# A gMLP layer on one core: two of the seven Strassen products of a pair of strips are computed by a second level

## The chip, the core and the metric

The kernel runs on one core of a Trainium2 chip. A core has a matmul engine (TensorE; PE in the profile, PEld its weight loads), a vector engine (DVE), a scalar engine (ACT), GpSimd (POOL), a sync engine (SP) that issues transfers, 16 DMA engines, an on-chip memory SBUF and accumulator banks in PSUM. The metric is the device time of one execution in microseconds (us), the median over runs.

## What is computed

One layer of the reference (DEPTH is 1, so only the first mixer runs), in float32, with x 1024 x 2048, E = 4096 inner channels, w_in 2048 x 12288, w_out 4096 x 2048:

```python
h = rmsnorm(x, g_in)
u, v, gate = split(h @ w_in, 3, axis=-1)
v = rmsnorm(gelu(v), v_gain)
vc = v.reshape(1, 8, 128, 8, 512)               # chunks of 128 positions, 8 groups of 512 channels
sv = einsum('gpq,bnqgc->bnpgc', w_s, vc) + b_s
y = gelu(u) * sv
out = rmsnorm(x + (y * silu(gate)) @ w_out, fnorm)
```

## The kernel before, in words

**Strassen.** h @ w_in is cut into 12 strips of two column groups of 512: strips 0 to 3 hold v (E columns, two groups each), strips 4 to 11 hold group g of u and group g of gate. A strip is a product of 2 x 2 blocks: rows of the 1024 positions in two halves, the 2048 input channels in two halves, the two column groups. It is done with 7 products in place of 8 (`IN_ORDER`; `A_OF` and `B_OF` name the sums of blocks of h and of w that a product takes). Each product is 4 *steps* of 256 input channels. A step combines and splits its weights in `feed`: `w_sum` (L112, vector engine, where two blocks are summed), `w_hi` (L88, scalar engine, the rounded value), `w_lo` (L89, vector engine, the remainder). It then does 24 matmuls of 128x128 on 128x512: two halves `u` of the channels, four row blocks `m`, and three products hi-hi, hi-lo, lo-hi for each (`mm3`, L102 to L104).

**Loads.** Strip 0 makes the hi and lo parts of h and of its sums from x and writes them to `a_dram` through POOL's queue; every later strip reads two of them of 512 KB for each step, and each block of w once (16 of 512 KB a strip), all through SP's queue. `prefetch` runs `LOADS` = 3 steps ahead, `feed` runs `AHEAD` = 2 steps ahead. What is really resident is set by slots: tiles of 128 x 1024 floats in the pools `big` (w_raw, a_hi, a_lo), `hl` (six: w_hi and w_lo of three steps), `sum` (three) and `ax` (the rest).

**The end of a product.** `end_of` puts the work on the four PSUM banks of a product into the list `soon` (U = M1 - M2 - M5, outputs c11 to c22, gelu or silu by `act`), and the rest (squares and gains of v, transposes of y) into `later`; `work` puts some of both behind the matmuls of each step. Blocks 12 and 21 go straight from the bank through `act`. From strip 4 on, spatial mixing of a group (`spatial_step` k = 0 to 10: load v, split it, matmuls `sv`, `scalar_tensor_tensor` L370, transposes L398 and writes of y) is spread over products 7 and 6 of its strip (k = 0 to 7) and product 1 of the next (k = 8 to 10). After the strips the `out` stage multiplies y by w_out in the same way, one level of seven products. A scheduler sets the order of instructions on each engine from the order of the program and what each needs.

Of the kernel before, what the change touches and what calls it, by code (L numbers as in the profile page):

```python
# [23 lines left out]
FIRST_ORDER = (5, 3, 6, 1, 2, 4, 7)  # L24
OUT_ORDER = (3, 5, 2, 4, 1, 7, 6)
# [7 lines left out]
def gmlp_kernel(ctx, tc, x, xT, g_in, w_in, gain, wsT, bsT, w_out, fnorm, out):  # L33
# [19 lines left out]
    SLOTS = {"big": 25, "hl": 6, "sum": 3, "ax": 16}  # L53
# [65 lines left out]
    steps = [("in", s, p, j) for s in range(len(strips)) for p in (IN_ORDER if s else FIRST_ORDER) for j in range(JI)]  # L119
# [7 lines left out]

    wraw, yraw, wparts, aparts = {}, {}, {}, {}
    hx = {}

    def load_w(step, block, us=None):
        kind, s, p, j = step
        mat, cols, n = (w_in, strips, JI) if kind == "in" else (w_out, outs, JO)
        key = (kind, s, 0 if kind == "in" else p, block, j)
        if key not in wraw or us is not None:
            k = ((block // 10 - 1) * n + j) * 2 * P
            col = cols[s][block % 10 - 1]
            if key not in wraw:
# [73 lines left out]
    def feed(i):  # L212
# [16 lines left out]
        raw = combine(B_OF[p], lambda b: load_w(step, b), "sum", "w_sum")  # L229
# [25 lines left out]
    def load_x(jj, h, us=None):  # L255

        if (jj, h) not in hx:
            hx[jj, h] = slot("big", "x_t")
# [149 lines left out]

    def products(i, banks, fresh, ms=range(4)):
# [10 lines left out]

    def advance(i):
        prefetch(i + LOADS)
        feed(i + AHEAD)
# [5 lines left out]
    i = 0  # L429
    before = None  # L430
    for s in range(len(strips)):
        is_v = s < NV
        g = s - NV
        a = (s - 1) % 2
# [256 lines left out]
```

## Time and profile before

| | |
|---|---|
| median of 3 runs | 2521.28 us (2520.66 to 2523.06) |
| the profiled execution | 2521.24 us, of which the span of instructions is 2519.2 us |
| granted TensorE clock, mean | 0.998 |
| matmuls (PE) | 99% of the span, 10948 instructions |
| vector engine, scalar engine, POOL | 61%, 36%, 9% |
| transfers | 685.09 MB, 272 GB/s in the mean |

The busy share says how much of the span an engine had an instruction under way; for the engine that is near 100% its number of instructions sets the time, for the others the waits do, and only where somebody waits for them.

### The profile page before, as it was taken

The numbers are of one execution on the slowest core, as the hardware profiler recorded it, in microseconds if no ns is written. First come the engines' busy times: TensorE is split into PE (matmuls) and PEld (weight loads), VectorE is DVE, ScalarE is ACT, GpSimd is POOL, SyncE is SP. The second block draws the span as 40 slices with busy tenths as digits, with TensorE's granted clock in tenths as the row PEclk, the third lists the DMA queues.
The fourth block names the chain that finished last, engine by engine and source line by source line (L and its number), as shares of the span: only waits on it lengthen the run. The fifth ranks groups of instructions, "written<-read, shape, count | busy, mean of one in ns | idle before, by whom it ended". The sixth has DMA issues, their size and how long they took to land.

```text
span 2519.2 us, 28981 instructions
## 1 busy us (share of the span) xinstructions
PE 2489.9 (99%) x10948; PEld 2055.3 (82%) x10948; DVE 1526.9 (61%) x1561; ACT 898.2 (36%) x1148; POOL 219.2 (9%) x386
## 2 busy tenths in 40 slices
PE   8999999999999999999999999999999999999998
PEld 6778888888888888888888888888888888888886
DVE  7984544546456464564645646456468664676795
ACT  6752433324333242332423324233243342232342
POOL 2220000000001001010010100101002110010010
PEclk9999999999999999999999999999999999999999
DMA  9896977959677687776877768777689865788885
GB/s 384 289 352 220 346 252 253 340 189 378 239 293 246 221 326 245 291 250 220 328 244 292 250 221 327 242 291 252 215 334 305 289 217 187 218 269 282 304 285 190
DMA packets 242922, 685.09 MB, mean 272 GB/s; under 512 B 22736, under 2 KB 22752, under 8 KB 242784
## 3 DMA queue, kind: packets, MB, share of 16 engines
q1 hardware_dynamic: 202160, 541.13, 60.7%
q0 software_dynamic: 40624, 142.12, 15.3%
q8 instruction: 86, 1.41, 0.2%
q14 instruction: 52, 0.43, 0.1%
HBM read 611.86 MB, written 71.30 MB: 271 GB/s over the span
## 4 chain that ended last, share of the span: by engine, by line
PE 93%; DMA 2%; issue 2%; POOL 1%; DVE 1%; ACT 0%; SPq 0%; POOLq 0%; ACTq 0%
PE m L102 23%; PE m L104 23%; PE m L103 23%; PE o L102 8%; PE o L104 8%; PE o L103 8%; DMA w_raw<-in_w_in 2%; PE sv L104 1%; PE sv L102 1%; PE sv L103 1%; DMA x_t<-in_xT 0%; DMA v<-c 0%; SPq L261 0%; POOL rx L287 0%; ACT sq_o L563 0%
## 5 line engine op out<-in xcount | busy, mean ns | idle before, releaser
L102 PE MATMUL m<-w_hi,a_hi 128*128 128x512 f32 x2688 | 1047.4, 390 | 14.0 <-ACT a_hi L88 8.4
L103 PE MATMUL m<-w_lo,a_hi 128*128 128x512 f32 x2688 | 1047.7, 390 | 1.4 <-DVE w_lo L89 1.4
L104 PE MATMUL m<-w_hi,a_lo 128*128 128x512 f32 x2688 | 1046.7, 390 | 1.7 <-DVE a_lo L89 1.7
L88 ACT ACTIVATE w_hi<-w_sum 128x1024 fp32r<-128x1024 f32 x320 | 338.7, 1059 | 906.1 <-PE m L103 643.7
L89 DVE TENSOR_TENSOR w_lo<-w_sum,w_hi 128x1024 fp32r<-128x1024 f32 x320 | 391.4, 1223 | 440.5 <-ACT w_hi L88 440.0
L102 PEld LDWEIGHTS m<-w_hi,a_hi 128*128 128x128 f32 x2688 | 505.0, 188 | 122.3 <-ACT a_hi L88 10.1
L104 PEld LDWEIGHTS m<-w_hi,a_lo 128*128 128x128 f32 x2688 | 505.0, 188 | 108.6 <-DVE a_lo L89 3.4
L103 PEld LDWEIGHTS m<-w_lo,a_hi 128*128 128x128 f32 x2688 | 505.1, 188 | 107.4 <-DVE w_lo L89 1.8
L112 DVE TENSOR_TENSOR w_sum<-w_raw 128x1024 f32<-128x1024 f32 x320 | 389.8, 1223 | 161.8 <-DMA w_raw<-in_w_in 147.6
L102 PE MATMUL o<-w_hi,a_hi 128*128 128x512 f32 x896 | 348.7, 389 | 0.8 <-DVE o L638 0.8
L104 PE MATMUL o<-w_hi,a_lo 128*128 128x512 f32 x896 | 348.6, 389 | 0.0
L103 PE MATMUL o<-w_lo,a_hi 128*128 128x512 f32 x896 | 348.6, 389 | 0.0
L89 DVE TENSOR_TENSOR w_lo<-w_raw,w_hi 128x1024 fp32r<-128x1024 f32 (+1 forms) x129 | 156.3, 1215 | 237.9 <-ACT w_hi L88 237.8
L88 ACT ACTIVATE w_hi<-w_raw 128x1024 fp32r<-128x1024 f32 (+1 forms) x129 | 136.1, 1055 | 453.6 <-PE m L103 341.6
L102 PEld LDWEIGHTS o<-w_hi,a_hi 128*128 128x128 f32 x896 | 168.2, 188 | 36.3 <-DVE o L638 1.5
L104 PEld LDWEIGHTS o<-w_hi,a_lo 128*128 128x128 f32 x896 | 168.2, 188 | 34.9
L103 PEld LDWEIGHTS o<-w_lo,a_hi 128*128 128x128 f32 x896 | 168.2, 188 | 34.9
L403 POOL DMA_DIRECT2D y<-y_t x128 | 74.0, 586 | 409.4 <-DVE y_t L398 405.7
L155 POOL DMA_DIRECT2D y_raw<-y x96 | 50.9, 531 | 511.4 <-DVE w_sum L112 206.7
L95 ACT ACTIVATE a_hi<-a_sum 128x1024 fp32r<-128x1024 f32 x40 | 42.3, 1058 | 102.6 <-DVE a_sum L112 102.6
L450 ACT ACTIVATE c<-m,rx 128x512 f32<-128x512 f32 x92 | 57.8, 682 | 51.0 <-PE m L104 51.0
L479 DVE TENSOR_TENSOR u<-u,m 128x1024 f32<-128x1024 f32 x46 | 56.1, 1219 | 31.4 <-PE m L104 29.9
(94 smaller groups left out, 1148.3 us busy)
## 6 DMA issues: line engine op xcount, KB each, us to landing
w_raw<-in_w_out SPq DMA_DIRECT2D x192, 512.0 KB, 7.5
w_raw<-in_w_in SPq DMA_DIRECT2D x191, 512.0 KB, 6.2
y_raw<-y POOLq DMA_DIRECT2D x96, 512.0 KB, 6.7
a_hi<-a_0h SPq DMA_DIRECT2D x77, 512.0 KB, 6.3
a_lo<-a_0l SPq DMA_DIRECT2D x77, 512.0 KB, 5.3
a_hi<-a_1h SPq DMA_DIRECT2D x77, 512.0 KB, 6.0
a_lo<-a_1l SPq DMA_DIRECT2D x77, 512.0 KB, 5.0
a_hi<-a_2h SPq DMA_DIRECT2D x77, 512.0 KB, 6.1
```

Of the source, the lines that this page charges most:

```text
L88: nc.scalar.activation(out=hi, in_=raw, func=AF.Copy)
L89: nc.vector.tensor_tensor(out=lo, in0=raw, in1=hi.bitcast(F32), op=ALU.subtract)
L95: nc.scalar.activation(out=hv, in_=rv_, func=AF.Copy)
L102: nc.tensor.matmul(out=acc, lhsT=ah, rhs=bh, start=start, stop=False, skip_group_check=on)
L103: nc.tensor.matmul(out=acc, lhsT=ah, rhs=bl, start=False, stop=False, skip_group_check=on)
L104: nc.tensor.matmul(out=acc, lhsT=al, rhs=bh, start=False, stop=stop, skip_group_check=on)
L112: nc.vector.tensor_tensor(out=s, in0=a, in1=b, op=ALU.add if of[1] > 0 else ALU.subtract)
L155: nc.gpsimd.dma_start(out=yraw[key], in_=y_dram[g][block // 10 - 1][b * P:(b + 2) * P].rearrange("(p u) t -> p u t", p=P))
L403: nc.gpsimd.dma_start(out=yd[n, :, :, q * P:(q + 1) * P], in_=yts[0][n][q * Q:(q + 1) * Q])
L450: nc.scalar.activation(out=d[:, c], in_=src[:, c], func=AF.Gelu_apprx_tanh if is_v or n == 0 else AF.Silu, scale=rx[half][:, at:at + 1])
L479: soon.append((1.2, lambda t=t: nc.vector.tensor_tensor(out=cs["u"][t], in0=cs["u"][t], in1=banks[t], op=ALU.subtract)))
```

## The change

Strips 0 and 1 stay as they were. From strip 2 on, strips are taken in pairs. Product 2 is (A21 + A22) B11 and product 5 is (A11 + A12) B22; for the two strips of a pair the left sides are the same, so the two products of a pair are one product of a 512 x 1024 matrix with a 1024 x 1024 one. It is cut into quarters and done with seven products (`deep` steps, two for each of the seven, 12 matmuls a step, `deep_product`). Their hi and lo parts of quarters are made once, in strip 1 (`whole`, `deep_parts`), and written to `d_dram` (28 writes of 512 KB). The results D2 and D5 stay in SBUF (`ax`). Then each strip of the pair has its five other products in the order 1, 4, 3, 7, 6, and `end_of` adds D2 and D5 in SBUF on the vector engine. Loads run ahead by `when`, in which a deep step counts a half. Block 11 of w is loaded again for product 6. The steps 8 to 10 of a mixing left over from the strip before stand at the first deep steps of product 2.

```diff
+DEEP = (2, 5)
+REST_ORDER = (1, 4, 3, 7, 6)
...
-    SLOTS = {"big": 25, "hl": 6, "sum": 3, "ax": 16}
+    SLOTS = {"big": 21, "hl": 6, "sum": 3, "ax": 20}
...
-    steps = [("in", s, p, j) for s in range(len(strips)) for p in (IN_ORDER if s else FIRST_ORDER) for j in range(JI)]
+    steps = [("in", s, p, j) for s in range(2) for p in (IN_ORDER if s else FIRST_ORDER) for j in range(JI)]
+    for s in range(2, len(strips), 2):
+        steps += [("deep", s, (p, q), j) for p in DEEP for q in IN_ORDER for j in range(JI // 2)]
+        steps += [("in", s + n, p, j) for n in range(2) for p in REST_ORDER for j in range(JI)]
...
-        key = (kind, s, 0 if kind == "in" else p, block, j)
+        key = (kind, s, 0 if kind == "in" and not (s > 1 and (p, block) == (6, 11)) else p, block, j)
...
+    def load_deep(step, block):
+        _, s, (p, q), j = step
+        return load_w(("deep", s + block % 10 - 1, p, 2 * (block // 10 - 1) + j), 11 if p == 2 else 22)
...
-        if kind == "in" and s > 0:
+        if kind == "deep" and j > 0:
+            aparts[i] = aparts[i - 1]
+        elif kind == "deep" or (kind == "in" and s > 0):
             parts = [slot("big", f"a_{l}", F32R) for l in ("hi", "lo")]
-            for t, d in zip(parts, a_dram[p, j]):
+            for t, d in zip(parts, d_dram[p] if kind == "deep" else a_dram[p, j]):
...
-        for c, at in enumerate((0, 1, 4, 6)):
+        for c, at in enumerate((0, 1, 4, 5)):
             if k == at:
                 load_v(g, c)
-        for c, at in enumerate((2, 3, 6, 8)):
+        for c, at in enumerate((2, 3, 6, 7)):
             if k == at:
                 prepare_spatial(g, c)
...
+    def whole(i):
...
+        raws[p, j] = slot("ax", "a_raw")
+        hi, lo = aparts[i]
+        nc.vector.tensor_tensor(out=raws[p, j], in0=hi.bitcast(F32), in1=lo.bitcast(F32), op=ALU.add)
+    def deep_parts(p, q):
+        of = A_OF[q]
...
+        if len(of) > 1:
+            both = slot("sum", "d_sum").rearrange("p a (b c) -> p (a b) c", c=HT2)
+            for j in range(2):
+                nc.vector.tensor_tensor(out=both[:, 2 * j:2 * j + 2], in0=block(of[0], j), in1=block(of[2], j),
+                                        op=ALU.add if of[1] > 0 else ALU.subtract)
+            split(both, hi, lo)
+        else:
+            for j in range(2):
+                split(block(of[0], j), hi[:, 2 * j:2 * j + 2], lo[:, 2 * j:2 * j + 2])
+        for t, d in zip((hi, lo), d_dram[p, q]):
+            nc.gpsimd.dma_start(out=d.rearrange("p a (b c) -> p (a b) c", c=HT2), in_=t.bitcast(F32))
...
+    def deep_product(i, bank, fresh):
...
+        for u in range(2):
+            for m in range(2):
+                t = slice(m * P, (m + 1) * P)
+                mm3(bank[:, m], ah[:, 2 * j + u, t], al[:, 2 * j + u, t], bh[:, u], bl[:, u],
+                    fresh and j == 0 and u == 0, j == 1 and u == 1, not fresh)
+    when = [0.0]
+    for step in steps:
+        when.append(when[-1] + (0.5 if step[0] == "deep" else 1.0))
+    fetched, fed = [LOADS], [AHEAD]
     def advance(i):
-        prefetch(i + LOADS)
+        while fetched[0] < len(steps) and when[fetched[0]] <= when[i] + LOADS:
+            prefetch(fetched[0])
+            fetched[0] += 1
         feed(i + AHEAD)
...
+                for j in range(JI // 2):
+                    advance(i)
+                    if n == 0 and s > NV:
+                        at = {(1, 0): 8, (1, 1): 9, (2, 0): 10}.get((q, j))
+                        if at:
+                            spatial_step(at, *before)
+                    deep_product(i, bank, fresh)
+                    work(0.1 if j else 0)
+                    i += 1
+                end_deep(p, q, bank)
...
+    def end_deep(p, q, bank):
+        if q == 1:
+            deep["u"] = slot("ax", "d_u")
+            soon.append((0, lambda u=deep["u"]: nc.scalar.activation(out=u, in_=bank, func=AF.Copy)))
+        elif q in (2, 5):
+            soon.append((1.2, lambda u=deep["u"]: nc.vector.tensor_tensor(out=u, in0=u, in1=bank, op=ALU.subtract)))
+        elif q in (4, 3):
+            d = deep[p, 21 if q == 4 else 12] = slot("ax", f"d{p}")
+            soon.append((0, lambda: nc.scalar.activation(out=d, in_=bank, func=AF.Copy)))
+        else:
+            u = deep["u"]
+            d = deep[p, 11 if q == 7 else 22] = slot("ax", f"d{p}") if q == 7 else u
+            soon.append((1.2, lambda: nc.vector.tensor_tensor(out=d, in0=u, in1=bank, op=ALU.add)))
...
+                if s > 1:
+                    n = s % 2 + 1
+                    d2, d5 = deep[2, 10 * (t + 1) + n], deep[5, 10 * (t + 1) + n]
+                    if p == 1:
+                        for block, d in ((11, d5), (22, d2)):
+                            c = slot("ax", f"c{block}_{t}")
+                            cs.setdefault(block, []).append(c)
+                            soon.append((1.2, lambda t=t, c=c, d=d: nc.vector.tensor_tensor(
+                                out=c, in0=banks[t], in1=d, op=ALU.subtract)))
+                    else:
+                        block = {4: 21, 3: 12, 7: 11, 6: 22}[p]
+                        if p in (4, 3):
+                            cs.setdefault(block, []).append(d2 if p == 4 else d5)
+                        def add(t=t, block=block):
+                            c = cs[block][t]
+                            nc.vector.tensor_tensor(out=c, in0=c, in1=banks[t], op=ALU.add)
+                            act(block, t, c)
+                        soon.append((1.2, add))
...
+            if s == 1 and p in DEEP:
+                for q in IN_ORDER:
+                    later.append((2.3, lambda p=p, q=q: deep_parts(p, q)))
...
```

A pair of strips issues 56 loads of w and 108 of h parts, where it issued 32 and 112. TensorE has 10708 matmuls, 420 `w_sum` and 507 `w_hi`/`w_lo` are made in place of 320 and 447.

The vector engine's rows, before, at products 5 and 4 of a strip (out<-in; names end in a running number):

```order
L89 TENSOR_TENSOR w_lo_6017<-w_raw_5786,w_hi_6016 128x1024
L89 TENSOR_TENSOR w_lo_6049<-w_raw_5625,w_hi_6048 128x1024
L112 TENSOR_TENSOR w_sum_6220<-w_raw_6178,w_raw_5661 128x1024
L89 TENSOR_TENSOR w_lo_6081<-w_raw_5663,w_hi_6080 128x1024
L479 TENSOR_TENSOR u0_5974<-u0_5974,m2_0_5976 128x1024
L112 TENSOR_TENSOR w_sum_6256<-w_raw_6214,w_raw_5736 128x1024
L89 TENSOR_TENSOR w_lo_6115<-w_raw_5738,w_hi_6114 128x1024
L479 TENSOR_TENSOR u1_5975<-u1_5975,m2_1_5977 128x1024
L89 TENSOR_TENSOR w_lo_6151<-w_raw_5788,w_hi_6150 128x1024
L89 TENSOR_TENSOR w_lo_6187<-w_sum_6184,w_hi_6186 128x1024
```

and of the changed kernel in product 5 of a deep stage, where it sums and splits for deep steps:

```order
L116 TENSOR_TENSOR w_sum_10166<-w_raw_9990,w_raw_9848 128x1024
L536 TENSOR_TENSOR d_u_10031<-d_u_10031,d5_5_10074 128x1024
L93 TENSOR_TENSOR w_lo_10123<-w_sum_10120,w_hi_10122 128x1024
L116 TENSOR_TENSOR w_sum_10185<-w_raw_10013,w_raw_9875 128x1024
L93 TENSOR_TENSOR w_lo_10142<-w_sum_10139,w_hi_10141 128x1024
L116 TENSOR_TENSOR w_sum_10212<-w_raw_9846,w_raw_10033 128x1024
L93 TENSOR_TENSOR w_lo_10169<-w_sum_10166,w_hi_10168 128x1024
L116 TENSOR_TENSOR w_sum_10231<-w_raw_9873,w_raw_10056 128x1024
L93 TENSOR_TENSOR w_lo_10188<-w_sum_10185,w_hi_10187 128x1024
L116 TENSOR_TENSOR w_sum_10258<-w_raw_10158,w_raw_10160 128x1024
L93 TENSOR_TENSOR w_lo_10215<-w_sum_10212,w_hi_10214 128x1024
L116 TENSOR_TENSOR w_sum_10277<-w_raw_10204,w_raw_10206 128x1024
```

Before, a step of 24 matmuls stands for each `w_lo`, and most of these read a `w_raw`; after, a step of 12 stands for each, most have a `w_sum`, and each sum stands two `w_lo` ahead of its own (`w_lo_10123` and `w_lo_10142` stand between `w_sum_10166` and `w_lo_10169`).

The vector engine where the mixing of one strip ends beside the next strip, before (in product 1 of the next strip; `u` L508 is of the next strip's accumulations, L459 forms u times gate):

```order
L89 TENSOR_TENSOR w_lo_6873<-w_sum_6870,w_hi_6872 128x1024
L508 TENSOR_TENSOR u0_5974<-u0_5974,m5_0_6108 128x1024
L508 TENSOR_TENSOR u1_5975<-u1_5975,m5_1_6109 128x1024
L89 TENSOR_TENSOR w_lo_6923<-w_sum_6920,w_hi_6922 128x1024
L459 TENSOR_TENSOR c21_0_6396<-c21_0_6396,u0_5974 128x1024
L459 TENSOR_TENSOR c21_1_6397<-c21_1_6397,u1_5975 128x1024
L89 TENSOR_TENSOR w_lo_6973<-w_sum_6970,w_hi_6972 128x1024
L89 TENSOR_TENSOR w_lo_7005<-w_raw_6749,w_hi_7004 128x1024
L370 SCALAR_TENSOR_TENSOR c21_0_6396<-sv1_1_0_7008,bs_sb_65,c21_0_6396 128x512 x2
```

and of the changed kernel, where the next is deep product 2 (L575 forms u times gate, L396 the product with sv):

```order
L93 TENSOR_TENSOR w_lo_9652<-w_raw_9479,w_hi_9651 128x1024
L575 TENSOR_TENSOR d2_7549<-d2_7549,c22_0_8965 128x1024
L575 TENSOR_TENSOR d_u_7337<-d_u_7337,c22_1_8967 128x1024
L93 TENSOR_TENSOR w_lo_9678<-w_raw_9519,w_hi_9677 128x1024
L396 SCALAR_TENSOR_TENSOR d2_7549<-sv3_1_0_9706,bs_sb_65,d2_7549 128x512
L93 TENSOR_TENSOR w_lo_9702<-w_raw_9481,w_hi_9701 128x1024
L396 SCALAR_TENSOR_TENSOR d2_7549<-sv3_1_0_9706,bs_sb_65,d2_7549 128x512
L396 SCALAR_TENSOR_TENSOR d_u_7337<-sv3_1_1_9707,bs_sb_65,d_u_7337 128x512 x2
L424 STREAM_TRANSPOSE y_t0_9754<-d2_7549 128x8x32
L424 STREAM_TRANSPOSE y_t1_9755<-d2_7549 128x8x32
L424 STREAM_TRANSPOSE y_t0_9754<-d2_7549 128x8x32
L93 TENSOR_TENSOR w_lo_9739<-w_raw_9521,w_hi_9738 128x1024
```

Here `w_lo_9652` and `w_lo_9678` are for the two steps of quarter product 2, `w_lo_9702` and `w_lo_9739` for those of 5. The same mixing rows stand between `w_lo` of steps half as long.

The scalar engine at the end of a v strip, before (L450 gelu, L324 square with its sum):

```order
L88 ACTIVATE w_hi_3644<-w_sum_3642 128x1024
L450 ACTIVATE u0_2730<-u0_2730,rx1_75 128x512 x2
L450 ACTIVATE u1_2731<-u1_2731,rx1_75 128x512 x2
L324 ACTIVATE sq_v_3712,ssv_71<-u0_2730 128x512 x2
L324 ACTIVATE sq_v_3718,ssv_71<-u1_2731 128x512 x2
L88 ACTIVATE w_hi_3684<-w_sum_3682 128x1024
L88 ACTIVATE w_hi_3728<-w_raw_3505 128x1024
```

and of the changed kernel, at the end of strip 1 and the start of the first deep stage:

```order
L92 ACTIVATE w_hi_2695<-w_sum_2693 128x1024
L92 ACTIVATE w_hi_2761<-w_raw_2589 128x1024
L566 ACTIVATE u0_1700<-u0_1700,rx1_75 128x512 x2
L566 ACTIVATE u1_1701<-u1_1701,rx1_75 128x512 x2
L350 ACTIVATE sq_v_2741,ssv_71<-u0_1700 128x512 x2
L350 ACTIVATE sq_v_2747,ssv_71<-u1_1701 128x512 x2
L92 ACTIVATE w_hi_2779<-w_raw_2639 128x1024
L534 ACTIVATE d_u_2795<-d2_1_2754 128x1024
L92 ACTIVATE w_hi_2803<-w_raw_2591 128x1024
```

In both, four gelus and four squares stand between two `w_hi`. The `w_hi` behind them, `w_hi_3684` before, is for a step of 24 matmuls; `w_hi_2779` is for the fourth deep step of 12.

## Rows read from the trace of the kernel before

**Rows 1.** The page: span, busy time of each engine, bytes moved.
```profile
span 2519.2 us, 28981 instructions
...
PE 2489.9 (99%) x10948; PEld 2055.3 (82%) x10948; DVE 1526.9 (61%) x1561; ACT 898.2 (36%) x1148; POOL 219.2 (9%) x386
...
DMA packets 242922, 685.09 MB, mean 272 GB/s; under 512 B 22736, under 2 KB 22752, under 8 KB 242784
```

**Rows 2.** Windows: length, then PE, PEld, DVE, ACT, POOL busy; clock, DMA share, GB/s.
```profile
0.00:150.00 150.00, 134.51 (x561) 106.13 (x562) 132.51 (x147) 102.80 (x138) 35.21 (x65) 1.00 0.89 332
150.00:308.00 158.00, 156.43 (x691) 129.20 (x690) 89.95 (x87) 55.70 (x86) 8.61 (x17) 1.00 0.81 302
1398.00:1554.00 156.00, 156.00 (x690) 129.18 (x689) 87.73 (x96) 51.53 (x61) 11.40 (x20) 1.00 0.74 266
```

**Rows 3.** Groups, whole span: busy us, mean ns | idle before, what ended it.
```profile
L103 PE MATMUL m<-w_lo,a_hi 128*128 128x512 f32 x2688 | 1047.7, 390 | 1.4 <-DVE w_lo L89 1.4
```

**Rows 4.** Timeline, PE: start us, us, instruction; first matmuls of two steps.
```profile
1000.15 0.39 PE L102 MATMUL m<-w_hi,a_hi 128*128 128x512 f32 x1
...
1005.59 0.39 PE L102 MATMUL m<-w_hi,a_hi 128*128 128x512 f32 x1
```

**Rows 5.** Timeline, ACT, beside it: in brackets the idle time before, and its end.
```profile
1004.89 1.06 ACT L88 ACTIVATE w_hi<-w_sum 128x1024 fp32r<-128x1024 f32 x1 [4.38 <-PE m L103]
1010.33 1.06 ACT L88 ACTIVATE w_hi<-w_sum 128x1024 fp32r<-128x1024 f32 x1 [4.38 <-PE m L103]
```

**Rows 6.** Groups by shape, whole span (columns as in rows 3).
```profile
L89 DVE TENSOR_TENSOR w_lo<-w_sum,w_hi 128x1024 fp32r<-128x1024 f32 x320 | 391.4, 1223 | 440.5 <-ACT w_hi L88 440.0
L112 DVE TENSOR_TENSOR w_sum<-w_raw 128x1024 f32<-128x1024 f32 x320 | 389.8, 1223 | 161.8 <-DMA w_raw<-in_w_in 147.6 <-DMA w_raw<-in_w_out 8.7
...
L479 DVE TENSOR_TENSOR u<-u,m 128x1024 f32<-128x1024 f32 x46 | 56.1, 1219 | 31.4 <-PE m L104 29.9
...
L398 DVE STREAM_TRANSPOSE y_t<-c 128x256 f32<-128x256 f32 x128 | 43.6, 408 | 0.0
L370 DVE SCALAR_TENSOR_TENSOR c<-sv,bs_sb,c 128x512 f32<-128x512 f32 x64 | 43.5, 743 | 0.0
...
L450 ACT ACTIVATE u<-u,rx 128x512 f32<-128x512 f32 x48 | 30.7, 711 | 0.1
...
L324 ACT ACTIVATE sq_v<-u 128x512 f32<-128x512 f32 x16 | 9.8, 618 | 0.0
...
L324 ACT ACTIVATION_READ_ACCUMULATOR sq_v<-u 128x1 f32 x16 | 3.0, 189 | 0.0
```

**Rows 7.** Timeline, DVE, a strip with mixing (columns as in rows 4, 5).
```profile
1087.21 1.22 DVE L89 TENSOR_TENSOR v_lo<-v_raw,v_hi 128x1024 fp32r<-128x1024 f32 x1
1088.35 1.22 DVE L89 TENSOR_TENSOR w_lo<-w_sum,w_hi 128x1024 fp32r<-128x1024 f32 x1
...
1094.16 2.72 DVE L370 SCALAR_TENSOR_TENSOR c<-sv,bs_sb,c 128x512 f32<-128x512 f32 x4
1096.80 2.72 DVE L398 STREAM_TRANSPOSE y_t<-c 128x256 f32<-128x256 f32 x8
...
1140.47 1.22 DVE L112 TENSOR_TENSOR w_sum<-w_raw 128x1024 f32<-128x1024 f32 x1 [8.15 <-DMA w_raw<-in_w_in]
```

**Rows 8.** Windows of the highest and a low transfer rate (columns as in rows 2).
```profile
40.00:60.00 20.00, 19.23 (x85) 15.60 (x85) 17.98 (x20) 11.60 (x14) 4.79 (x9) 1.00 1.03 410
220.00:240.00 20.00, 20.00 (x90) 16.57 (x89) 9.36 (x8) 4.25 (x4) 0.00 (x0) 1.00 0.51 176
...
1201.00:1214.00 13.00, 13.00 (x59) 10.78 (x58) 6.12 (x5) 4.22 (x4) 0.00 (x0) 1.00 1.02 409
```

**Rows 9.** Waits: who waits for what: us in total, times, longest.
```profile
ACT w_hi L88 <- PE m L103: 985.2, 249, 7.0
DVE w_lo L89 <- ACT w_hi L88: 677.8, 277, 4.5
...
DVE w_sum L112 <- DMA w_raw<-in_w_in: 147.6, 57, 9.2
```

More of the change, by code (lines that the diff above doesn't have):

```diff
@@ L126, in gmlp_kernel @@
               for p in IN_ORDER for j in range(JI)}
+    d_dram = {(p, q): [dram.tile([P, 2, C], F32, tag=f"d{p}_{q}{l}", name=f"d{p}_{q}{l}") for l in "hl"]
+              for p in DEEP for q in IN_ORDER}
     wraw, yraw, wparts, aparts = {}, {}, {}, {}
@@ L228, in feed @@
             aparts[i] = aparts[i - JO]
-        raw = combine(B_OF[p], lambda b: load_w(step, b), "sum", "w_sum")
+        if kind == "deep":
+            raw = combine(B_OF[p[1]], lambda b: load_deep(step, b), "sum", "w_sum")
+        else:
+            raw = combine(B_OF[p], lambda b: load_w(step, b), "sum", "w_sum")
         wparts[i] = [slot("hl", f"w_{l}", F32R) for l in ("hi", "lo")]
@@ L257, in load_x @@
         if (jj, h) not in hx:
-            hx[jj, h] = slot("big", "x_t")
+            hx[jj, h] = slot("ax" if h == 1 and jj >= JI else "big", "x_t")
         src = xT[jj * 2 * P:(jj + 1) * 2 * P, h * HT:(h + 1) * HT].rearrange("(u p) c -> p u c", p=P)
@@ L510, in end_of @@
                     soon.append((1.2, last))
-        for p in IN_ORDER if s else FIRST_ORDER:
-            fresh = p in (1, 2, 5)
+        if s > 1 and s % 2 == 0:
+            deep_stage(s, b)
+        for p in FIRST_ORDER if s == 0 else IN_ORDER if s == 1 else REST_ORDER:
+            fresh = p in (1, 2, 5) or (s > 1 and p in (4, 3))
             if s == 0:
@@ L516, in gmlp_kernel @@
             if fresh:
-                sets[p] = bank_set(b if p == (2 if s else 1) else a, f"m{p}")
-            chain = sets[{4: 2, 7: 2, 3: 5, 6: 5}.get(p, p)]
+                second = (1,) if s == 0 else (2,) if s == 1 else (4,)
+                sets[p] = bank_set(b if p in second else a, f"m{p}")
+            chain = sets[p if fresh else {4: 2, 7: 2, 3: 5, 6: 5}[p] if s < 2 else {7: 4, 6: 3}[p]]
             for j in range(JI):
                 advance(i)
-                if is_v and i % n_first == 6:
+                if is_v and (p, j) == (3, 0):
                     load_gains()
                 if not is_v and p in (7, 6):
-                    spatial_step(4 * IN_ORDER.index(p) + j - 20, *mixing)
-                elif p == 1 and s > NV:
+                    spatial_step(j if p == 7 else 4 + j, *mixing)
+                elif p == 1 and s > NV and s % 2:
                     spatial_step(8 + j, *before)
                 products(i, chain, fresh)
+                if s == 1 and p in DEEP:
+                    whole(i)
                 if s == 0:
@@ L532, in gmlp_kernel @@
             end_of(p, chain)
-            if p == 2 and s == NV:
+            if s == 1 and p in DEEP:
+                for q in IN_ORDER:
+                    later.append((2.3, lambda p=p, q=q: deep_parts(p, q)))
+            if s == 1 and p == 6:
                 work_all()
-                finish_rv()
         before = mixing
@@ L548, in init_acc @@
             return
-        acc[s, block] = [slot("big", f"o{block}_{t}") for t in range(2)]
+        acc[s, block] = [slot("ax" if s == 1 and block in (11, 22) else "big", f"o{block}_{t}") for t in range(2)]
         col = outs[s][block % 10 - 1]
```

39 lines of the change are left out of this document (33 added, 6 removed).

## The prediction

> **What bounds the kernel now.** I read the totals first. Matmuls fill 2489.9 of the span of 2519.2 us, the vector engine 61%, the scalar engine 36% [rows 1]. Then the stretches: outside the first strip TensorE is busy without a gap (156.00 of 156 us) at a granted clock of 1.00, that is 2.4 GHz, so there is nothing but matmuls to remove [rows 2]. The groups say that no matmul waits: all 2688 of line 103 together waited 1.4 us [rows 3]. Last the price of one matmul: the busy mean of 390 ns overlaps the next one; what counts is start to start. A step of 24 matmuls begins at 1000.15 and the next at 1005.59, so 5.44 us a step and 226.7 ns a matmul [rows 4].
>
> What feeds a step is just in time by design. The three pairs of `hl` slots let the scalar engine start w_hi of step i+3 when step i is done: it starts every 5.44 us and waits 4.38 us for the matmuls each time [rows 5]. From there w_hi (1.06) and w_lo (1.22) take 2.3 us [rows 5, 6], and TensorE still has two steps, 10.9 us, in hand. That cover is what the change halves.
>
> **The change part by part.** *Matmuls.* Products 2 and 5 of two strips were 2 x 2 x 96 = 384 matmuls; by the second level they are 2 x 7 x 24 = 336. Five pairs: 240 fewer, 10948 to 10708, each still 128x512. 240 x 226.7 ns = **54.4 us** off a path that is nothing but matmuls. The profiled execution took 2521.24 us (2.0 us outside its span; the median of the runs is 2521.28), so without any new stall **2466.8 us**.
>
> *Feeding a deep step.* A deep step has 12 matmuls (2.72 us) but wants a whole w_hi and w_lo, and 10 of the 14 in each product of quarters want a w_sum. Cover behind the slot falls from 10.9 to 5.44 us, less 2.3 us for w_hi and w_lo: 3.1 us to spare. Vector engine in a step with a sum: 1.22 + 1.22 = 2.45 us of 2.72, plus 4 times per 14 steps a 1.22 us difference with a bank. The order of its rows shows a w_sum of a later step ahead of each w_lo, so the sum, w_hi and w_lo of one step don't stand in one chain. Per product 24 + 4 instructions of 1.22 us [rows 6] are 34.2 us against 38.1: it fits, at 90%. Back to back they cost less: v_lo starts at 1087.21 and the next w_lo 1.14 us later, though each is 1.22 us long [rows 7]. By that 31.9 of 38.1 us. I cost clean deep steps at nothing; the cover is this margin, and if it is gone each sum-step costs what the chain is longer (rival D).
>
> *The three stages with a mixing left over* (pairs after strips 5, 7 and 9). Beside deep product 2 the vector engine finishes the strip before: 8 products with sv, 16 transposes, a v_lo and six 1.22 us operations. Between w_lo of the first deep step and that of the fourteenth I count 29 operations of 1024 columns, 8 scalar_tensor_tensors and 16 transposes. At the spacing of [rows 7] (1.14; four in 2.72; eight in 2.72): 33.1 + 5.4 + 5.4 = 43.9 us. Allowed are 13 x 2.72 + 2.72 for sv = 38.1 us plus the lead at the start: w_hi of the first deep step is free 13.6 us before that step (sv and two whole steps), so w_lo is there 11.2 us ahead. 49.3 against 43.9 leaves 5 us, from which DVE's own waits for banks come off. At full busy times (1.22, 0.74, 0.41: 47.9) 1.4 us are left and waits turn into stalls. Bounds 0 and 6 us a pair; I take 0.5, nearest to the spacing seen: **1.5**.
>
> The Trainium skill, "VectorE: DVE Perf Modes", section "The DRAIN you can't avoid", says that the next vector operation does not start until the pipe of the one before has emptied. By it the busy times would add up whole, 47.9 us, and the three stages would be on the edge: an estimate of 2 to 3 us of stall each, 2476 in all instead of 2474. The row above, with starts 1.14 us apart, disagrees with it here.
>
> *Entry of the first deep stage.* Strip 1 ends with u0, u1 and the scalar engine's gelus and squares of them, which stand ahead of w_hi of the fourth deep step. Chain from the last matmul of the strip: first difference 1.22, second overlapping to 2.36, four activations of 0.71 from 1.3 on but the second pair not before 2.4 (to 4.2), four squares with their accumulator reads (0.62 + 0.19 each) to 7.4, w_hi 8.5, w_lo 9.7 us, some 9.8 with the hand-overs. By then three deep steps, 8.16 us, are done (all durations [rows 6], the difference at the 1.22 of a sum): **1.6 us** of stall, once. Before, the same rows stood ahead of a w_hi with two whole steps and more in hand.
>
> *Strip 1.* `whole` and `deep_parts` add 8 + 12 x 2 halves and 14 w_lo-like operations: some 40 us on the vector engine, which was at 57% there [rows 2]; covered by 5.44 us steps. Their 28 writes of 512 KB are 14.7 MB. The strip moved 302 GB/s x 158 us = 47.7 MB [rows 2]; 62.4 MB at the 410 GB/s that saturated stretches reach [rows 8] take 152 us of the strip's 152. But the writes come after product 2, where the stretch 220 to 240 moved 176 GB/s [rows 8], and only 5 slots of `big` are free for the next a parts there (16 of 21 hold w). Bounds 0 and 36 us (14.7 MB with no cover); I take **2**, since the valley is as wide as the writes.
>
> The Trainium skill, "DMA: Bandwidth & Descriptors", section "Bandwidth", holds that for HBM to SBUF the HBM side binds at about 358 GB/s. By it 62.4 MB want 174 us and strip 1 alone would lose about 20 us (2492). Our rows move 410 GB/s on this lone core, so the sum goes by those.
>
> *Loads of the pairs.* A pair needed 32 w and 112 a loads, now 56 and 108: 20 more, 52.4 MB over five pairs; with the 685.09 of today [rows 1] and the writes 752 MB in some 2470 us, 305 GB/s. That is three quarters of 410. What can bite is one late load: in each strip w_sum stood up to 8.15 us waiting for w_raw [rows 7], 147.6 us in all [rows 9], and no matmul paid. In a deep stage the cover is 3.1 us plus what w_sum runs ahead. Bounds 0 and 5 us (8.15 less 3.1) for each of ten products; I take **1** in all, because w loads of a deep stage are issued several steps before their sum. In strip 0 three w loads start later (9 free slots before x leaves): bounds 0 and 4, I take **1**.
>
> Sum: 2466.8 + 1.5 + 1.6 + 2 + 1 + 1 = 2473.9, so **2474 us**.
>
> **The rivals.** *A, the forecast:* TensorE keeps nearly all; 2466 to 2486.
> *B: the vector engine becomes the bound in part.* Each deep stage is at 84 to 90% and any idle time before w_sum or w_lo now reaches TensorE. For it: 677.8 us of w_lo waiting for w_hi today [rows 9]; against: those waits have matmuls behind them (w_hi waits 985.2 us for TensorE), they are slack, not work. Price: 6 us in each of three stages, and 1 us in each of ten products: 28 us more than the floor, 2495. It decides from 3.1 us of lateness in one deep step.
> *C: the transfers bind.* Writes of strip 1 uncovered, 36 us for the 2: 2508. The skill's 358 GB/s is the mild form of it. Against: 410 GB/s seen, and the valley.
> *D, slower: sum, w_hi and w_lo run as one chain in deep steps.* 1.22 + 1.06 + 1.22 and two hand-overs, 3.8 us, against 2.72: 1.1 us x 100 sum-steps = 110 us, 2577. It decides from 54.4 / 100 = 0.54 us a sum-step. Against: the rows' order. For it: only three `sum` slots and three `hl` pairs, and in a deep stage everything waits on everything.
>
> **How the numbers follow.** A 0.68, B 0.20, C 0.04, D 0.06, gains eaten to within 0.2% 0.02. 0.2% (5 us) is about what a measurement of this kernel can tell from no change. Faster: A + B + C = 0.92; same 0.02; slower 0.06. The range takes A and most of B: 2465 (floor, less noise) to 2499.
>
> **What would show it.** Right: 10708 matmuls starting 226.7 ns apart in the deep stages, matmul idle time under 10 us more than now, the first lost 1.5 us at the fourth deep step of strip 2 behind w_hi, the vector engine near 75% over the span and near 90% in deep product 2. Wrong: matmuls of d2 or d5 waiting on w_lo in most steps (B, D), on a_hi or behind w_raw (C); DMA share at 1.0 through the end of strip 1 with matmuls waiting.

## The result, and the profile after

The changed kernel takes 2501.32 us (median of 4, 2498.71 to 2503.95) against 2521.82: a ratio of 0.9919, interval [0.9901, 0.9936]. It is faster, as forecast, but by 20 us (0.8%) and not 47; 2501 lies just outside the range, which ended at 2499. The page of the profiled execution (2498.71 us, the shortest of the four), as in [rows 1]:

```profile
span 2497.0 us, 29261 instructions
...
PE 2442.9 (98%) x10708; PEld 2012.3 (81%) x10708; DVE 1831.9 (73%) x1847; ACT 986.1 (39%) x1236; POOL 234.8 (9%) x414
...
DMA packets 276720, 752.24 MB, mean 301 GB/s; under 512 B 24784, under 2 KB 24800, under 8 KB 276576
```

The matmuls are the 10708 that were counted and the bytes the 752 MB. So the missing 27 us are stalls. Who the matmuls wait for (us in total, times, longest):

```profile
PE d L107 <- DVE w_lo L93: 16.4, 7, 8.5
PE m L106 <- ACT a_hi L92: 9.3, 3, 7.9
PE m L107 <- DVE w_lo L93: 8.4, 2, 7.0
PE m L106 <- ACT c L630: 4.5, 2, 2.9
```

The second row stands before the first matmul, as before the change. Where the others lie is read from the matmuls' starts: where two neighbours begin more than 0.26 us apart, I add what is over 0.227 us and call it *lost*. Before, 18.3 us are lost in all; after, 52.2. The 33.9 more less the 54.4 saved leave 20.5 us up to the last matmul. Behind it this execution is 2.3 us shorter than the one before the change, so the two profiled executions differ by 22.5 us; that the medians differ by 20.5 too is chance. The losses lie at four places:

| us lost | before | after |
|---|---|---|
| strip 0, 58 to 80 us | 3.7 | 6.1 |
| end of strip 1, start of the first deep stage (330 and 357 us) | 0 | 9.0 + 11.0 |
| three deep stages with a mixing left over (992, 1301, 1608 us) | 0 | 3.0 + 3.8 + 2.8 |
| rest (start, strip 0, out stage) | 14.6 | 16.5 |

The timeline of the matmul engine at the second place, and at the third:

```profile
330.37 0.80 PE L107 MATMUL m<-w_lo,a_hi 128*128 128x512 f32 x1 [6.97 <-DVE w_lo L93]
330.96 0.63 PE L108 MATMUL m<-w_hi,a_lo 128*128 128x512 f32 x1
331.39 0.63 PE L106 MATMUL m<-w_hi,a_hi 128*128 128x512 f32 x1
...
357.28 0.79 PE L107 MATMUL d<-w_lo,a_hi 128*128 128x512 f32 x1 [8.50 <-DVE w_lo L93]
...
992.28 0.50 PE L107 MATMUL d<-w_lo,a_hi 128*128 128x512 f32 x1 [1.39 <-DVE w_lo L93]
996.42 0.50 PE L107 MATMUL d<-w_lo,a_hi 128*128 128x512 f32 x1 [1.10 <-DVE w_lo L93]
```

The matmuls name `w_lo`, but it is not the vector engine that is short. Its own timeline there:

```profile
313.29 1.21 DVE L643 TENSOR_TENSOR c<-u,m 128x1024 f32<-128x1024 f32 x1
327.96 1.22 DVE L116 TENSOR_TENSOR w_sum<-w_raw 128x1024 f32<-128x1024 f32 x1 [13.46 <-DMA w_raw<-in_w_in]
329.10 1.22 DVE L93 TENSOR_TENSOR w_lo<-w_sum,w_hi 128x1024 fp32r<-128x1024 f32 x1
...
988.74 1.23 DVE L116 TENSOR_TENSOR w_sum<-w_raw 128x1024 f32<-128x1024 f32 x1 [4.05 <-DMA w_raw<-in_w_in]
```

It sits 13.46 us in front of a `w_sum` of a later step whose `w_raw` has not landed, with the `w_lo` that the matmuls wait for behind it. The windows (columns as in [rows 2]) show what the transfers do:

```profile
296.00:352.00 56.00, 45.81 (x193) 37.15 (x192) 35.49 (x41) 24.18 (x46) 8.00 (x15) 0.93 1.03 414
320.00:330.00 10.00, 3.40 (x16) 2.47 (x14) 2.04 (x2) 0.00 (x0) 0.00 (x0) 0.87 1.03 410
330.00:340.00 10.00, 9.63 (x34) 7.86 (x35) 10.00 (x15) 8.52 (x21) 2.13 (x4) 0.79 1.04 409
350.00:360.00 10.00, 2.72 (x6) 2.15 (x7) 7.56 (x8) 5.00 (x13) 0.20 (x1) 0.56 1.03 402
380.00:400.00 20.00, 20.00 (x90) 16.57 (x89) 17.54 (x15) 9.26 (x9) 0.00 (x0) 1.00 0.91 342
960.00:970.00 10.00, 10.00 (x46) 8.28 (x45) 9.87 (x15) 4.25 (x4) 0.89 (x2) 1.00 0.36 114
980.00:990.00 10.00, 10.00 (x46) 8.29 (x45) 5.81 (x6) 4.80 (x5) 0.53 (x1) 1.00 1.03 410
```

For 56 us the transfers run at their 410 GB/s, and in the mixing stage a valley of 114 GB/s is followed by a burst of 410. A load then lands late. The issues from 280 to 360 us (times, KB each, median us to landing):

```profile
w_raw<-in_w_in SPq DMA_DIRECT2D x9, 512.0 KB, 17.5
...
d_7h<-d_hi POOLq DMA_DIRECT2D x1, 512.0 KB, 13.4
...
a_hi<-d_3h SPq DMA_DIRECT2D x1, 512.0 KB, 18.6
```

From 290 to 316 us, while parts of quarters are written, the loads of SP (q1) and the writes of POOL (q0) each get about half of the rate (packets, MB, share of the 16 engines):

```profile
q1 hardware_dynamic: 1519, 5.51, 53.9%
q0 software_dynamic: 1382, 5.07, 47.8%
```

By the landing times in the trace, the loads land 2.5 us apart from 294 to 324 us, and 1.3 us apart from 326 us on, when the last of these writes has landed.

### The profile page after: what moved, and what is told of

Its sections match the earlier page's. It is cut to its first block, busy times and chain, and to the rows that moved or that the text cites. A ratio compares the mean times of both kernels' runs of the same rounds, so it can differ in the third digit from the quotient of the medians.

```text
span 2497.0 us, 29261 instructions
## 1 busy us (share of the span) xinstructions
PE 2442.9 (98%) x10708; PEld 2012.3 (81%) x10708; DVE 1831.9 (73%) x1847; ACT 986.1 (39%) x1236; POOL 234.8 (9%) x414
## 3 DMA queue, kind: packets, MB, share of 16 engines
q8 instruction: 85, 1.39, 0.2%
## 4 chain that ended last, share of the span: by engine, by line
PE 85%; DMA 7%; DVE 4%; issue 2%; ACT 1%; SPq 1%; POOL 0%; POOLq 0%; ACTq 0%; DVEq 0%
PE m L107 16%; PE m L108 16%; PE m L106 16%; PE o L107 7%; PE o L106 7%; PE o L108 7%; DMA w_raw<-in_w_in 5%; PE d L107 4%; PE d L108 4%; PE d L106 4%; DMA a_lo<-a_2l 1%; DVE w_lo L93 1%; DVE w_sum L116 1%; DMA x_t<-in_xT 1%; PE sv L107 1%
## 5 line engine op out<-in xcount | busy, mean ns | idle before, releaser
L106 PE MATMUL m<-w_hi,a_hi 128*128 128x512 f32 x2048 | 799.2, 390 | 16.7 <-ACT a_hi L92 9.3
L107 PE MATMUL m<-w_lo,a_hi 128*128 128x512 f32 x2048 | 799.7, 391 | 8.4 <-DVE w_lo L93 8.4
L108 PE MATMUL m<-w_hi,a_lo 128*128 128x512 f32 x2048 | 798.6, 390 | 1.7 <-DVE a_lo L93 1.7
L93 DVE TENSOR_TENSOR w_lo<-w_sum,w_hi 128x1024 fp32r<-128x1024 f32 x420 | 513.0, 1221 | 274.4 <-ACT w_hi L92 272.5
L116 DVE TENSOR_TENSOR w_sum<-w_raw 128x1024 f32<-128x1024 f32 x420 | 511.3, 1221 | 198.6 <-DMA w_raw<-in_w_in 181.5
L106 PEld LDWEIGHTS m<-w_hi,a_hi 128*128 128x128 f32 x2048 | 385.3, 188 | 100.1 <-ACT a_hi L92 10.9
L108 PEld LDWEIGHTS m<-w_hi,a_lo 128*128 128x128 f32 x2048 | 385.4, 188 | 83.7 <-DVE a_lo L93 3.4
L107 PE MATMUL d<-w_lo,a_hi 128*128 128x512 f32 x560 | 219.7, 392 | 16.4 <-DVE w_lo L93 16.4
L106 PE MATMUL d<-w_hi,a_hi 128*128 128x512 f32 x560 | 218.6, 390 | 0.0
L108 PE MATMUL d<-w_hi,a_lo 128*128 128x512 f32 x560 | 218.6, 390 | 0.0
L108 PEld LDWEIGHTS o<-w_hi,a_lo 128*128 128x128 f32 x896 | 168.2, 188 | 34.9
```

The source lines that it names most:

```text
L93: nc.vector.tensor_tensor(out=lo, in0=raw, in1=hi.bitcast(F32), op=ALU.subtract)
L106: nc.tensor.matmul(out=acc, lhsT=ah, rhs=bh, start=start, stop=False, skip_group_check=on)
L107: nc.tensor.matmul(out=acc, lhsT=ah, rhs=bl, start=False, stop=False, skip_group_check=on)
L108: nc.tensor.matmul(out=acc, lhsT=al, rhs=bh, start=False, stop=stop, skip_group_check=on)
L116: nc.vector.tensor_tensor(out=s, in0=a, in1=b, op=ALU.add if of[1] > 0 else ALU.subtract)
```

## The experiments

All are edits of the changed kernel. Losses are worked out as above; one execution each, unless an interval is given. What leaves work out says so in its expectation. Where a fence has a line of an earlier experiment, its edit stands on top of that one.

**No writes of the parts of quarters.**
```diff
-            for t, d in zip(parts, d_dram[p] if kind == "deep" else a_dram[p, j]):
+            for t, d in zip(parts, a_dram[p[0], IN_ORDER.index(p[1]) % JI] if kind == "deep" else a_dram[p, j]):
...
-        for t, d in zip((hi, lo), d_dram[p, q]):
-            nc.gpsimd.dma_start(out=d.rearrange("p a (b c) -> p (a b) c", c=HT2), in_=t.bitcast(F32))
```


> The 28 writes of parts of quarters in strip 1 are left out, and deep steps read parts of the same size that strip 0 wrote (so their products are of other data); the sums and splits that make the parts are still done. The changed kernel loses 9.0 us of matmul time at the end of strip 1 and 11.0 us at the start of the first deep stage. Theory W (the writes, bunched at the end of strip 1, crowd out the loads): both are gone, at most 3 us stay, so about 2482 us. Rival P (the deep stage's own prefetch does it, at twice the rate and in fewer slots): at least 10 us stay, 2490 us or more. Rival V (the extra vector work of strip 1 does it): nothing changes, about 2500 us.

Measured 2488.29 us. The first deep stage loses 3.8 in place of 20.1 us, a little over the 3 expected: theory W, and not the vector work, which is still done. From 290 to 316 us SP's queue now has the whole rate, and its loads land 1.3 us apart:

```profile
q1 hardware_dynamic: 3381, 10.45, 102.5%
```

The edit also makes the deep steps load other parts; but between 280 and 365 us no wait of SP in the changed kernel names a write, so it was not the order of write and load that held them. The mixing stages now lose 14.1 where they lost 9.5, so their loss has another cause. Of the 14.1, 2.5 us are matmuls at the lower clock behind a stall of 3.9 us at 977 us; why that one was longer is open.

**Doubled work behind the steps of strip 1.**
```diff
-                work(2.3 if s else 1.4)
+                work((4.6 if s == 1 else 2.3) if s else 1.4)
```


> In strip 1 the work put behind each step is doubled (4.6 in place of 2.3 us), so the parts of quarters are made and written earlier, and the squares of v as well. Theory W: the writes end before the loads of the deep stage begin, the 20 us at the end of strip 1 and after fall to under 8, so about 2487 us. Rival P: no change, 2498 to 2504 us. Rival V: the denser vector work makes w_lo of strip 1 late, new stalls there, 2502 us or more.

Measured 2496.66 us, a miss for all three. Nothing is lost any more at the deep stage, but 11.6 us at 295 us, in strip 1. The vector engine there:

```profile
279.07 1.23 DVE L93 TENSOR_TENSOR w_lo<-w_sum,w_hi 128x1024 fp32r<-128x1024 f32 x1 [1.19 <-ACT w_hi L92]
289.64 2.50 DVE L351 TENSOR_TENSOR c<-c,gain_b 128x512 f32<-128x512 f32 x4 [9.35 <-DMA gain_b<-in_gain]
```

The load of gains now stood in POOL's queue behind the writes.

**Parts of deep stages loaded two full steps after their w.**
```diff
-        if kind == "deep" and j > 0:
-            aparts[i] = aparts[i - 1]
-        elif kind == "deep" or (kind == "in" and s > 0):
+        if kind == "in" and s > 0:
...
+        while fetched_a[0] < len(steps) and when[fetched_a[0]] <= when[i] + 1:
+            prefetch_a(fetched_a[0])
+            fetched_a[0] += 1
```


> In deep stages the two loads of parts of h for a product of quarters are issued two full steps later than the loads of w for it. Theory Q (the w_raw that the vector engine waits for stands in the queue behind parts that are wanted later): the 9.5 us that the three stages with a mixing lose fall to under 3, and of the 20 us at the first stage some 8 go, so about 2485 us. Rival R (the rate itself or the slots bind, not the order): no gain, within 3 us of 2500 us. Rival L: the parts now come late, matmuls wait for a DMA in each product of quarters, 2510 us or more.

Measured 2483.38 us. The mixing stages lose nothing, the first deep stage 13.6: theory Q, at its size. No matmul of a deep stage waits for a part. Of the 13.6 us 2.2 are at the fourth deep step, behind w_hi and w_lo.

**Without the second half of the mixing of strips 5, 7 and 9.**
```diff
-                        if at:
+                        if at and False:
```


> The second half of the mixing of strips 5, 7 and 9 is left out (their 36 matmuls, 12 scalar_tensor_tensors, 24 transposes, 24 writes of y and 3 of the loads of v that stand beside deep product 2; the out stage reads the first half of another group in its place). Leaving out 36 matmuls alone is worth 36 x 226.7 ns = 8.2 us. Theory M (the mixing makes the loads of the deep stage late): the 9.5 us of stalls of these three stages are gone too, so about 2482 us. Rival T (the change from product 2 to product 5 stalls by itself): they stay, about 2492 us.

Measured 2482.54 us. The three stages lose nothing, the first one 20.1 as before: the mixing it is. (The loads of v in that burst belong to the next strip and were not left out; but at the first of these stages they are issued from 951.8 us on in place of 977.7, ahead of the burst.) Which part of the mixing is open here.

**Pace with early gains; then with later parts too; and later parts without the writes.**
```diff
-                if is_v and (p, j) == (3, 0):
+                if is_v and (p, j) == ((1, 0) if s == 1 else (3, 0)):
```


> The doubled work of strip 1 again, and the load of gains for strip 1 is issued at its first product, so that it no longer stands behind the 14 writes of parts of product 5 (in the run before, the vector engine waited 9.35 us for it with w_sum behind it). Theory W (writes late in strip 1 crowd out the loads): the stall of 11.6 us at 295 us is gone and none comes at the first deep stage but the chain of gelus and squares, under 4 us; the mixing stages keep their 10 to 13 us; about 2485 us. Rival P (the deep stage's own prefetch): 8 us or more stay between 290 and 370 us, 2491 us or more.

Measured 2485.24 us: 4.9 us stay at 290 us, the mixing stages lose 9.9. Theory W.

> Both remedies: strip 1 paced and its gains early, and the parts of h of deep stages loaded two steps later than their w. If the two causes are separate, both sums go: of the 13.6 us that the later loads alone left at the first deep stage under 4 us stay, the mixing stages lose nothing, 2483.4 - 10 = about 2473 us. If the denser vector work of strip 1 or the later parts cost something of their own, 2478 us or more.

Measured 2476.24 us: 5.0 us at 290 us, none in mixing stages. The two remedies add up to within 3 us; the dense vector work keeps its 5 us.

> No writes of parts of quarters (deep steps read parts that strip 0 wrote, so their products are of other data), and the parts loaded two steps later than w. What stays at the first deep stage is not transfers: by the prediction's chain of gelus and squares 1.6 us, by the run without writes alone 3.8 us. About 2471 to 2474 us. Rival P: if the deep stage's own loads were the cause, some 8 us of the 13.6 stay, 2478 us.

Measured 2473.36 us: the first deep stage loses nothing at all, not even the 1.6 us of gelus and squares.

**Slots of `big` back to 23, with later parts.**
```diff
-    SLOTS = {"big": 21, "hl": 6, "sum": 3, "ax": 20}
+    SLOTS = {"big": 23, "hl": 6, "sum": 3, "ax": 18}
```


> Later parts as before, and slots of big back from 21 to 23, those of ax from 20 to 18. Theory S (strip 0 loses 3 to 4 us more than before the change since SP waits for slots of big with the w loads): the loss between 58 and 80 us falls from 7.9 to 4 or 5 us, about 2480 us. Rival: fewer slots of ax make the vector or the scalar engine wait in mixing or in the writes of strip 1, 2484 us or more.

Measured 2485.50 us. Strip 0 loses 3.0 in place of 7.9, theory S; the first deep stage loses 10.4, but the out stage 12.3, so the sum is a miss, at the rival's number.

**Parts one step later; and, apart from that, no loads of v.**
```diff
-        while fetched_a[0] < len(steps) and when[fetched_a[0]] <= when[i] + 1:
+        while fetched_a[0] < len(steps) and when[fetched_a[0]] <= when[i] + 2:
...
-        spatial["v", c] = slot("ax", "v_raw")
-        nc.gpsimd.dma_start(out=spatial["v", c], in_=v_dram[g][h][:, 2 * t:2 * t + 2])
+        spatial["v", c] = ws_sb.rearrange("p (u g) c -> p u (g c)", u=2)
```


> The parts of h of deep stages are loaded one full step later than their w in place of two. Theory Q (what counts is how many loads of parts stand ahead of the w_raw that the vector engine waits for): part of the gain, the three mixing stages lose 1 to 6 us (9.5 with none, 0 with two steps), about 2486 to 2492 us. If two steps only helped since they moved the loads past the writes of y, one step gives nothing, 2498 us.

Measured 2484.52 us: the mixing stages lose 1.2, the first deep stage 16.3. One step does most of the work of two.

> The 32 loads of v for the mixing are left out (16.8 MB; the mixing takes the mixing matrices in place of v, so y is of other data); all its other work stays, and the parts are loaded with their w as in the changed kernel. Three loads of v fall into the 20 us in which a mixing stage's loads are late; at 410 GB/s they take 3.8 us. Theory C (the transfers of the mixing crowd out the w_raw): the 9.5 us of the three stages fall to under 2, about 2490 us. Theory O (its work on the matmul and vector engines holds slots, so the loads start late): 7 us or more stay, 2496 us or more.

Measured 2490.75 us: the mixing stages lose 0.95 in place of 9.5 us, the first deep stage 20.0. Theory C: the valley is still there (121 GB/s from 960 to 970 us), but without 3.8 us of other transfers in the burst behind it the w loads land in time. Leaving the loads out also frees slots of `ax`; but at the first of these stages the three w loads that were late are issued 25.9, 28.9 and 29.9 us behind its first matmul, as in the changed kernel (26.0, 28.9, 29.9), and land at 36.4, 40.3 and 41.7 in place of 38.9, 44.2 and 45.6 us. So the rate is what changed, not the time of issue.

**Half the extra pace; the same with 22 slots of `big` and 19 of `ax`.**
```diff
-                work((4.6 if s == 1 else 2.3) if s else 1.4)
+                work((4.6 if s == 1 and j % 2 else 2.3) if s else 1.4)
```


> As with both remedies, but the work of strip 1 is doubled only behind every second step. Expected: the 5.0 us that the doubled work lost at 287 us shrinks to under 2 and the writes still end before the deep stage's loads, 2471 to 2474 us. If half the pace is too slow for the writes, the stalls come back at 320 to 360 us, 2478 us or more.

Measured 2475.19 us: 3.7 us at 290 us, 2.0 at 348, the fourth deep step. The 5.0 did not fall under 2, and 1 us of gain is no more than single executions vary by.

> The same with 22 slots of big and 19 of ax. With 23 and 18 the loss of strip 0 between 58 and 80 us fell from 7.9 to 3.0 us and the end of the out stage lost 9 us. Expected: one slot gives 2 to 5 us in strip 0, and the out stage loses less than 3 us: 2468 to 2473 us. If the out stage needs all 20, 2475 us or more.

Measured 2475.12 us: strip 0 loses 3.2, the first deep stage 2.8, but the out stage 9.8; a miss.

**Slots and two accumulators alone; everything together; later parts timed.**
```diff
-        acc[s, block] = [slot("ax" if s == 1 and block in (11, 22) else "big", f"o{block}_{t}") for t in range(2)]
+        acc[s, block] = [slot("ax" if s == 1 and block == 11 else "big", f"o{block}_{t}") for t in range(2)]
```


> The changed kernel with 23 slots of big and 18 of ax, and two of the four accumulators of the out stage that it had moved to ax back in big. Theory S (strip 0 loses since big has fewer slots): the loss between 58 and 80 us falls from 6.1 to 3 or 4 us; the out stage loses under 2 us; the first deep stage and the mixing stages keep some 20 and 10 us. About 2498 us in a profiled run. Rival: the out stage's wait comes from ax in general, it loses 5 us or more, 2503 us.

Measured 2480.29 us, 18 us less than expected: strip 0 loses 2.4, the out stage 2.3, and the mixing stages 1.1 and the first deep stage 14.6. So what the out stage lacked were slots for accumulators, and two more slots of `big` are nearly as good for the mixing stages as the later loads.

> Work of strip 1 doubled behind every second step, its gains early, parts of deep stages loaded two steps after their w, 23 slots of big and 18 of ax with two accumulators back in big. The stalls over those of the kernel before would be 29.0 - 18.3 = 10.7 us without the slots; 4 to 5 of them are strip 0's and go. Floor 2466.8 us and some 6: about 2472 us, ratio to before 0.979 to 0.982. If the out stage still lacks slots, 2477 us.

Measured 2465.53 us (2464.87 to 2466.10, 4 runs), ratio 0.9781, interval [0.9766, 0.9795]: the fastest of all, 36 us under the changed kernel and 6 under what was expected. Its windows from strip 1 into the first deep stage, and its largest waits of the matmul engine:

```profile
280.00:360.00 80.00, 79.89 (x352) 65.71 (x351) 64.45 (x64) 41.80 (x69) 6.09 (x12) 1.00 1.03 402
385.00:405.00 20.00, 20.00 (x90) 16.57 (x89) 19.16 (x18) 9.57 (x10) 0.00 (x0) 1.00 1.01 371
```

```profile
PE m L106 <- ACT a_hi L92: 8.3, 3, 7.3
PE m L108 <- DVE a_lo L93: 1.7, 4, 0.6
PE m L106 <- ACT c L578: 1.6, 1, 1.6
```

The transfers run at their limit for 80 us, and the vector engine is 96% busy in a deep stage, while the matmuls lose 0.4 us in the first of these windows and nothing in the second. In all 18.9 us are lost, as before the change.

> The later loads of parts alone, timed in rounds. The look gave 2483.4 us, 15 us under the profiled run and 18 under the median of the changed kernel: 2482 to 2488 us, ratio to before 0.985 to 0.987. If that look was only at the low end of what the entry's stall makes it vary, 2490 us.

Measured 2483.53 us (4 runs), ratio 0.9851, interval [0.9835, 0.9867]: as in the single execution.

## Why the prediction was wrong

**The matmuls: right.** 240 fewer, 54.4 us; with the added stalls removed the kernel takes 2465.5, the sum without new stalls was 2466.8.

**Feeding a deep step: right.** Clean deep steps cost nothing. From 380 to 400 us the vector engine is busy 17.54 of 20 us, 88%, and the matmuls 20.00. Rival D did not come, and rival B not by the engine that it named.

**Strip 1: the step that failed.** "I take 2, since the valley is as wide as the writes." The bounds were 0 and 36, and 20.1 came. The valley was read at 220 to 240 us, where the writes of product 2 would go. Those of product 5 are issued from 284 to 311 us, one product of quarters about every 4.5 us, among the loads of the last steps and those of the deep stage. In the stretch 296 to 352 the kernel before moves 326 GB/s,

```profile
296.00:352.00 56.00, 56.00 (x249) 46.37 (x248) 28.16 (x27) 21.23 (x35) 2.66 (x5) 1.00 0.88 326
```

which leaves 84 of 410, or 4.7 MB in 56 us, for 7.3 MB of writes and the doubled rate of deep loads. I should have placed each write before taking the low end. Of the 20.1 us 16 go with the writes, and 6.5 with the order of loads alone; without the writes and with the later order nothing is left. So rival C, with a chance of 0.04, was the one that came, at a little over half of its price.

The Trainium skill, "DMA: Bandwidth & Descriptors", section "Bandwidth", has the HBM side bind at about 358 GB/s; an estimate by it was 2492 in all, nearer to 2501 than mine. The same section gives that figure as a core's share when both cores of the HBM domain stream, and 425 GB/s as measured on a core alone; the trace lies near the latter: 414 GB/s over 56 us, and 402 over 80 us with 0.4 us lost. So its size was near by luck; the cause was when the transfers came.

**The mixing stages: mechanism wrong, and the size.** 1.5 us, reckoned from the vector engine; 9.5 came (9.9 to 14.1 in the three experiments on the writes and the pace of strip 1). That engine waits for `w_raw` (4.05 us at 988.74) when the matmuls stall. Slots come free late in the mixing (SP waits up to 7.5 us for one between 930 and 980 us; without the second half of the mixing the w loads are issued 2.7 to 5.6 us earlier, counted from the stage's first matmul), so the loads come in one burst, in which loads of v and writes of y share the rate; and `w_raw` stands in the queue behind parts wanted later. Leaving out the mixing, its loads of v, or moving the parts back takes nearly all of it away (0, 0.95, 0), and two more slots too (1.1). So the loads miss by only a few us, and each of these makes up for it.

The rule on the emptied pipe that the prediction takes from the Trainium skill, "VectorE: DVE Perf Modes", section "The DRAIN you can't avoid", is not the whole of it: the section adds that an operation that is not held starts earlier. The starts 1.14 us apart agree with that, and it decided nothing here.

**Loads: misplaced.** "I take 1 in all, because w loads of a deep stage are issued several steps before their sum." Issued they were, but in a full queue that lead is worth little: 17.5 us to landing. The bound (5 us for each product, though [rows 9] has a wait of 9.2 us and not only 8.15) would have held the mixing stages' 9.5. **Strip 0:** 1 forecast, 2.5 came at 58 to 80 us (6.14 less 3.66). In the runs with 21 slots of `big`, strip 0 unchanged, this stretch loses 4.3 to 8.7 us, so the 2.5 is at the low side. Between 20 and 80 us SP waits 34.9 us for `w_sum` to free slots, where it waited 22.2 before (12.6 and 9.6),

```profile
SPq L156 <- DVE w_sum L116: 34.9, 4, 16.7
```

and with 23 slots and the accumulators moved it waits 24.0 us and the loss is 2.4, less than the 3.7 before.

**Entry chain: right mechanism and place, the size varies.** 1.6 us forecast. In the changed kernel larger stalls come before it and hide all but 0.3. Where they are taken away the fourth deep step waits behind w_hi and w_lo, as forecast: 2.2 us without the writes (with 1.6 of matmuls at the lower clock behind it, the 3.8 above), 2.2 with later parts,

```profile
354.64 0.50 PE L106 MATMUL d<-w_hi,a_hi 128*128 128x512 f32 x1 [0.94 <-ACT w_hi L92]
355.90 0.50 PE L107 MATMUL d<-w_lo,a_hi 128*128 128x512 f32 x1 [0.76 <-DVE w_lo L93]
```

2.0 with half the extra pace, 0.4 in the kernel with all remedies and none in three others. Where nothing holds up the vector engine, w_lo of that step is done 8.15 us behind the first deep matmul, and the three deep steps before it take 8.16: the chain was reckoned 1.6 us too long. Without the writes a `w_sum` that waited 2.85 us for its `w_raw` stood ahead of it on the vector engine.

By terms, in the changed kernel: 2 became 20.1, 1.5 became 9.5, strip 0's 1 became 2.5, 1.6 became 0.3 within the 20.1, the 1 for loads lies in the 9.5, and 1.9 came elsewhere. What stays open: why the loss differs by some us from run to run of the same kernel (the changed kernel's runs spread over 5.2 us, those of the kernel before over 2.4). One part of it is the clock, as the last section shows.

## What to carry to other kernels

A change that halves the time between operands halves the lateness that a load may have: list each load and write of the stretch in order of issue, with its slot, before a low end of a bound is taken. Where a wait names an engine, read what that engine waited for: here a sum for a later step stood in front of the remainder that was due. Loads whose user comes last go last in the queue: that alone, or two slots more with two accumulators moved, brought back 15 us or more of the 27 missing.

## What was not expected of the hardware

From issue to landing a load of 512 KB takes 3.3 to 4.7 us in a quiet stretch (220 to 240 us before the change, 176 GB/s) and 17.5 us (median of nine w loads) to 20 us when the stretch is at 410 GB/s. Most of that is the queue: in the traces before and after, SP never has more than eight loads under way at once, and they land one after another, 1.3 us apart when they have the whole rate (10.3 us for eight, at 309 us without the writes) and 2.5 us apart beside writes that take half of it (20.3 us, at 297 us in the changed kernel). So a saturated stretch shows itself as latency long before it shows as a gap (80 us at 402 GB/s and 0.4 us lost).

The granted clock fell to its lower level, 1.2 GHz, with each long idle time of the matmul engine: 0.87 in the window in which 6.97 us of idle time begin, 0.79 in the next, 0.56 at the second one (8.50 us). Matmuls behind it start 0.43 us apart (330.96, 331.39) in place of 0.227. Of the 20.1 us lost there, 20.1 - 6.97 - 8.50 = 4.6 come on top of the idle time. A stall at the full clock has something on top too, 0.27 us at 992 us (1.66 lost, 1.39 idle), so some 4 us are the clock's.

A stall of 1 to 2 us, as at 992 us, shows no such matmuls in the changed kernel, but it can. With later parts alone, the first deep stage has three stalls of 0.8 to 1.5 us within 5 us in both traces of that kernel. In one the clock stays at 1.00; in the other it falls, and seven matmuls behind the last stall start 0.43 us apart, 1.6 us in all (columns as in [rows 2]):

```profile
350.00:362.00 12.00, 9.39 (x39) 7.24 (x40) 10.10 (x11) 9.24 (x16) 1.59 (x3) 1.00 1.03 413
350.00:362.00 12.00, 9.31 (x32) 6.67 (x31) 8.66 (x10) 9.30 (x17) 1.59 (x3) 0.86 1.03 413
```

So one kernel can take 1.6 us more or less by the clock alone.
